# A hybrid attention layer on one core: the attention's work given out in pieces of one bank, and the q/k transposes spread over the gates' matmuls

## The chip, the core and the metric

The kernel runs on one core of one Trainium2 chip. The metric is the time of the whole launch in microseconds (us); lower is better. The kernel before took 1259.9 us, the median of three runs (1257.29 to 1260.52).

The engines are named as the profile names them: PE does matmuls (PEld loads their weights), DVE and ACT do element-wise work and read the matmuls' results, POOL does element-wise work on the core's own memory (SBUF), and SP issues nearly all transfers (DMA). Each has a queue of instructions and takes them in order. Matmul results stand in eight banks of 2 KB per partition (PSUM).

## The reference

One decoder layer over a sequence of 2048 tokens with a width of 1024, in float32: RMS norm, one input projection, two attention mixers with a SiLU gate each, an output projection and a residual.

```python
hdn = rmsnorm(x, norm_gain[i])
proj = jnp.einsum("bsd,de->bse", hdn, w_in[i])
q_a, k_a, v_a, g_a, q_b, k_b, v_b, g_b = jnp.split(proj, split_at, axis=-1)
# A: 8 query heads, 2 key heads: causal window of 128, with a learned sink per head
q_a = rope(rmsnorm(q_a, q_norm_a), pos); k_a = rope(rmsnorm(k_a, k_norm_a), pos)
o_a = banded_attention(q_a, k_a, v_a, A_WINDOW - 1, sinks) * jax.nn.silu(g_a)
# B: 8 heads, each under the patterns (128,1), (512,4), (2048,16), merged by denominators
q_b = rope(rmsnorm(q_b, q_norm_b), pos); k_b = rope(rmsnorm(k_b, k_norm_b), pos)
o_b = dilated_attention(q_b, k_b, v_b) * jax.nn.silu(g_b)
x = x + jnp.einsum("bse,ed->bsd", jnp.concatenate([o_a, o_b], -1), w_out[i])
```

## The kernel before, in words

**Stages and slots.** `STAGES` (L26) lists eight stages: four pairs of heads of mixer B, two groups of four heads of mixer A, and two column halves of the output projection. Each is cut into four slots of 512 tokens, a slot into two halves of 256. `proj(si, sb)` (L246) does the projection of one slot: for each half two groups of 8 x 3 matmuls for q, k and v (`pj`, tiles of 128x384), then the gates (8 x 3 matmuls per group, the second loop, L319). Each float32 product is three matmuls, of high and low parts (`mm3`, L241): weights `wh`, `wl`, activations `xh`, `xl`, gate weights `wgh`, `wgl`. ACT makes the high part and DVE or POOL the low one. In the last slot of a stage the next stage's weights are loaded into three staging buffers `stg` (L118, L131) and split by ACT and DVE (L104, L105).

**After a group of q, k, v**: `norm_rope` (L406) reads `pj` with ACT (squares, v) and DVE (rotary products t1, t2, and V at L311); POOL adds t1 and t2 (L431). `norm_factors` (L434) makes the norm factor `fac` on POOL (L437, L182). `norm_split` (L441) multiplies by it on DVE (L447) and splits into `hl` on ACT and POOL (L456 to L459). `finish` (L342) transposes `hl` on PE (`qk_transposes`: L475, L485, L490, L499), copies the results by ACT to Q, KK and `klz` (L477, L478, L502), and for B writes them to DRAM from the second half on (qd, kd, ld). Then it puts the slot's attention units in `pending`. `finish` is put in `deferred` at the end of a half and run in the next half, after the second group's matmuls (L305).

**Attention units.** A unit is one head on 512 queries: the windows of A and B (`window_unit`, `pair_units`), and for B the residue classes of the dilated pattern (`units_D`), which load q, k and v back from DRAM in another order (`load`). A unit has steps: scores (q times k, two or three banks `sc`; DVE adds the mask and takes the row maximum, ACT makes P, the exponentials, with row sums), transposes of P (banks `pt`; ACT copies the high part `pth`, DVE makes the low part `ptl`, both at `split_p`, L572), pv (the products of P with V, bank `po`, high parts, then low ones; ACT and DVE take the result), and after. `sc`, `pt`, `po` and `pj` have two banks each. After a dilated unit of the second head, row factors go to DRAM (rD) and come back spread over partitions (`Rb`, one buffer, L890); POOL then does four operations of 128x512: L899 (waits for the first `Rb`), L904 (waits for the second), L905, L906. These are put in `late`, with a count of steps to wait. A's `final` does the like (rA, L686, L688).

**What sets the order.** `proj` is a generator: it yields a cost after each 3 or 6 matmuls. The main loop (L968) calls `advance()` as often as the attention's share of cost asks for. `advance` (L931) moves the `late` counts on by one and gives out one step of one unit, in rounds over the units in flight: the oldest unit's step first, and of the newest its scores. The framework takes the order in which the code emits instructions as a priority and then orders each engine's queue by a timeline of its own.

Of the kernel before, what the change touches and what calls it, by code (L numbers as in the profile page):

```python
# [9 lines left out]
F32 = mybir.dt.float32  # L10
# [23 lines left out]
def hybrid_layer(ctx, tc, xT, xn, x, wB, wA, wO, ng, gains, sinks, rot, masks, ident, out):  # L34
# [211 lines left out]
    def proj(si, sb):  # L246
# [22 lines left out]
        for half in range(2):  # L269
# [8 lines left out]
            for tt in range(2):  # L278
# [40 lines left out]
            for gc in range(ngc):  # L319
                pg = ps.tile([128, 256], F32, name="pt" if early else "pj", bufs=2)  # L320
                for c in range(KC):
# [7 lines left out]
                    yield 330  # L329
                z = G[si, sb][gc][:, :, 2 * half:2 * half + 2, :]  # L330
# [185 lines left out]
    def proj_out(si, sb, wq, wg, last):  # L516
# [4 lines left out]
        for half in range(2):  # L521
# [6 lines left out]
            for tt in range(2):  # L528
# [20 lines left out]
                while deferred:  # L549
                    yield from deferred.pop(0)()  # L550
# [12 lines left out]

    def evac_o(po, dst):
# [11 lines left out]
    def window_scores(si, sb, h, nb, l):  # L576
# [4 lines left out]
        P = wk.tile([128, 4, 256], F32, name="P")  # L581
        for b in range(2):
# [19 lines left out]
    def window_unit(si, sb, h, stats, dst, after):  # L602
        s = {}

        def scores():
            s["p"] = window_scores(si, sb, h, *stats)
# [4 lines left out]
        def transposes():  # L611
            f0 = sb == 0
            cur0 = (0, 0) if f0 else (0, 1)
            n1, n2 = pt_slot()
            sp = spec
            s["n"], s["sp"] = (n1, n2), sp
            pt = ps.tile([128, 4, 128], F32, name="pt", bufs=2)
            for b, a in enumerate((cur0, (1, 0), (1, 1), (2, 0))):
                nc.tensor.transpose(pt[:, b, :], blk(*a), idf)
            split_p(pt, n1, n2)  # L620
# [7 lines left out]
        def pv():  # L628
            po = ps.tile([128, 512], F32, name="po", bufs=2)
# [7 lines left out]
            for hl in range(2):  # L637
                seq.append((v(0), n[hl][:, 0:2, :], 0))
                seq.append((v(1), n[hl][:, 2:4, :], 128))
                if sb > 0:  # L640
                    seq.append((v(-1), sp[hl][:, 1:6:4, :], 0))
                seq.append((v(2), sp[hl][:, 2:4, :], 256))
                seq.append((v(3), sp[hl][:, 0:5:4, :], 256))
            for n_, (a, b, o) in enumerate(seq):
                nc.tensor.matmul(po[:, o:o + 256], a, b, start=n_ == 0, stop=n_ == len(seq) - 1, skip_group_check=True)  # L645
            evac_o(po, dst)
# [393 lines left out]
```

## Time and profile before

| | |
|---|---|
| median of three runs | 1259.9 us |
| profiled execution, its own time | 1261.51 us |
| profiled execution, span from first to last instruction | 1259.4 us |
| PE busy, matmuls | 1174.8 us, 93%, 8328 |
| DVE, ACT, POOL busy | 850.7, 834.7, 680.4 us |
| mean granted clock of PE | 0.969 |
| DMA: moved, mean rate | 220.98 MB, 175 GB/s |

The page of the profile has a chain of waits (what ended last, followed back), groups of instructions by line, and the waits of each engine: whom it waited for, in total, how often, and the longest. In a row of the timeline the number in brackets is the engine's idle time ahead of the instruction, with what ended it. The granted clock is the share of full speed at which PE was allowed to run.

### The profile page before, as it was taken

How to read it: one execution, taken by the hardware profiler on the slowest of the kernel's cores; microseconds unless marked ns; L12 is line 12 of the kernel's file. 1: busy time of each engine (PE TensorE's matmuls, PEld its weight loads, DVE VectorE, ACT ScalarE, POOL GpSimd, SP SyncE). 2: the span in 40 equal slices, each digit the busy share in tenths (PEclk: the TensorE clock that was granted, in tenths of full speed). 3: DMA queues.
4: the chain of work that ended last, by engine and by line, in shares of the span. 5: the costliest groups of instructions: out<-in, count | busy, mean ns of one | idle time of the engine just before them, and what ended most of it. 6: DMA issues, size and time to landing. Idle time of an engine off the chain costs nothing.

```text
span 1259.4 us, 25438 instructions
## 1 busy us (share of the span) xinstructions
PE 1174.8 (93%) x8328; PEld 1141.3 (91%) x8328; DVE 850.7 (68%) x2288; ACT 834.7 (66%) x2418; POOL 680.4 (54%) x788
## 2 busy tenths in 40 slices
PE   6898979899899798899998999999999999999899
PEld 5898979899799798888997999898899998999898
DVE  5676768678677678776777788789868877522221
ACT  6477868678677687676777677677776776522221
POOL 4886734566645574536576567565655554333122
PEclk9899989999899899899998999999999999999999
DMA  7454677877687667687775764545333225566561
GB/s 215 120 166 127 193 226 212 229 200 212 182 250 207 210 190 201 189 244 204 199 210 172 228 203 143 150 137 167 114 97 94 80 89 165 163 192 211 166 191 69
DMA packets 196883, 220.98 MB, mean 175 GB/s; under 512 B 34312, under 2 KB 143632, under 8 KB 196752
## 3 DMA queue, kind: packets, MB, share of 16 engines
q1 hardware_dynamic: 196752, 219.37, 59.3%
q8 instruction: 66, 1.08, 0.4%
q14 instruction: 65, 0.53, 0.1%
HBM read 164.44 MB, written 54.86 MB: 174 GB/s over the span
## 4 chain that ended last, share of the span: by engine, by line
PE 55%; DMA 16%; DVE 10%; ACT 8%; POOL 6%; issue 3%; SPq 2%; POOLq 0%; ACTq 0%; DVEq 0%
PE pj L244 39%; DMA xs<-in_xT 3%; DMA Rb<-rD 2%; DMA stg<-in_wB 2%; PE po L849 2%; DMA stg<-in_wO 2%; DMA stg<-in_wA 2%; PE sc L590 1%; PE sc L591 1%; PE po L645 1%; PE pt L828 1%; PE po L735 1%; PE pt L719 1%; ACT P L599 1%; DVE ptl L574 1%
## 5 line engine op out<-in xcount | busy, mean ns | idle before, releaser
L244 PE MATMUL pj<-wh,xh 128*128 128x384 f32 (+1 forms) x1008 | 332.8, 332 | 12.2 <-ACT wh L104 5.5
L244 PE MATMUL pj<-wl,xh 128*128 128x384 f32 (+1 forms) x1008 | 334.4, 332 | 0.8 <-DVE wl L102 0.7
L244 PE MATMUL pj<-wh,xl 128*128 128x384 f32 (+1 forms) x1008 | 333.4, 331 | 1.3 <-DVE xl L157 1.3
L157 POOL TENSOR_TENSOR xl<-xs,xh 128x512 fp32r<-128x512 f32 x158 | 210.3, 1341 | 146.3 <-ACT xh L155 136.6
L155 ACT ACTIVATE xh<-xs 128x512 fp32r<-128x512 f32 x252 | 154.5, 629 | 123.6 <-PE pj L244 100.6
L244 PEld LDWEIGHTS pj<-wh,xh 128*128 128x128 f32 x1008 | 194.0, 193 | 15.7 <-ACT wh L104 5.8
L244 PEld LDWEIGHTS pj<-wl,xh 128*128 128x128 f32 x1008 | 194.8, 193 | 3.2 <-DVE wl L102 1.1
L244 PEld LDWEIGHTS pj<-wh,xl 128*128 128x128 f32 x1008 | 194.4, 193 | 3.0 <-DVE xl L157 1.6
L574 DVE TENSOR_TENSOR ptl<-pt,pth 128x512 fp32r<-128x512 f32 (+3 forms) x232 | 142.0, 619 | 35.5 <-ACT pth L573 31.8
L244 PE MATMUL pj<-xh,wgh 128*128 128x256 f32 x496 | 147.7, 298 | 17.9 <-DVE V L311 12.0
L244 PE MATMUL pj<-xh,wgl 128*128 128x256 f32 x496 | 145.8, 294 | 0.0
L244 PE MATMUL pj<-xl,wgh 128*128 128x256 f32 x496 | 145.4, 293 | 0.0
L573 ACT ACTIVATE pth<-pt 128x512 fp32r<-128x512 f32 (+3 forms) x232 | 123.1, 543 | 23.1 <-PE pt L719 8.1
L431 POOL TENSOR_TENSOR t<-t,t 128x256 f32<-128x256 f32 (+1 forms) x96 | 78.1, 814 | 77.9 <-DVE t L422 57.2
L244 PEld LDWEIGHTS pj<-xh,wgh 128*128 128x128 f32 x496 | 97.8, 197 | 19.7 <-ACT klz L502 5.9
L244 PEld LDWEIGHTS pj<-xl,wgh 128*128 128x128 f32 x496 | 97.8, 197 | 0.6
L244 PEld LDWEIGHTS pj<-xh,wgl 128*128 128x128 f32 x496 | 97.4, 196 | 0.9 <-DVE wgl L105 0.2
L814 ACT ACTIVATE P<-P,scD 128x256 f32<-128x256 f32 (+3 forms) x128 | 71.6, 560 | 33.6 <-DVE scD L813 32.9
L157 DVE TENSOR_TENSOR xl<-xs,xh 128x512 fp32r<-128x512 f32 x94 | 76.9, 823 | 21.1 <-ACT xh L155 20.5
L447 DVE TENSOR_TENSOR t<-t,fac 128x256 f32<-128x256 f32 (+1 forms) x96 | 67.4, 710 | 30.8 <-POOL fac L182 23.7
L182 POOL TENSOR_TENSOR fac<-un,mhalf 128x8 f32<-128x8 f32 (+1 forms) x48 | 85.4, 1779 | 2.5
L813 DVE CUSTOM_DVE_ANT_0 P<-sc,mk 128x256 f32<-128x256 f32 (+3 forms) x128 | 61.1, 484 | 32.2 <-PE sc L809 31.5
(188 smaller groups left out, 3082.8 us busy)
## 6 DMA issues: line engine op xcount, KB each, us to landing
xs<-in_xT SPq DMA_DIRECT2D x94, 512.0 KB
xs<-mx SPq DMA_DIRECT2D x32, 512.0 KB
vd<-V SPq DMA_DIRECT2D x64, 128.0 KB
qd<-qc SPq DMA_DIRECT2D x32, 256.0 KB
TT<-tab SPq DMA_DIRECT2D x32, 256.0 KB
cv<-vd SPq DMA_DIRECT2D x32, 256.0 KB
cq<-qd SPq DMA_DIRECT2D x32, 256.0 KB
ck<-kd SPq DMA_DIRECT2D x64, 128.0 KB
```

The costliest lines, as they stand in the source:

```text
L155: nc.scalar.activation(h, f, AF.Copy)
L157: eng.tensor_tensor(l, f, f32(h), op=OP.subtract)
L182: nc.gpsimd.tensor_tensor(y, u, mhalf.to_broadcast([128, n]), op=OP.pow)
L244: nc.tensor.matmul(o, a, b, start=first and n == 0, stop=last and n == 2, skip_group_check=True)
L431: nc.gpsimd.tensor_tensor(t1[:, :n], t1[:, :n], t2[:, :n], op=OP.add)
L447: nc.vector.tensor_tensor(t1v, t1v, fac[:, tt, :, None].to_broadcast([128, nh, 64]), op=OP.mult)
L573: nc.scalar.activation(hi, pt, AF.Copy)
L574: nc.vector.tensor_tensor(lo, pt, f32(hi), op=OP.subtract)
L590: nc.tensor.matmul(sc[:, j, :], q[h // 2][:, h % 2, i, :], kw, start=True, stop=False)
L813: nc.vector.tensor_tensor_reduce(pd, o[:, :m], m2[:, 512 - m:], -0.125, BIG, OP.add, OP.min, nb)
L814: nc.scalar.activation(pd, pd, AF.Exp, bias=nb, scale=-1.0, accum_out=l)
L849: nc.tensor.matmul(po[:, o:o + w], a, b, start=n_ == 0, stop=n_ == len(seq) - 1, skip_group_check=True)
```

## The change

`finish` is now a generator of which `fin_step()` takes one part at a time: four parts for a half of B (two banks of q/k transposes, the bank of low parts of k, the end), taken after every second group of gate matmuls instead of all at once after the second q/k/v group. What is left is taken before `norm_split`. In the output stages it is taken between the matmuls too.

A unit's step is now a list of parts of one bank each (`parts`): scores 2 (dilated: 3), transposes 2 (3), pv 2 (high parts, low parts). `advance` gives out one part. It makes up a round as: pv and after of the older units, then two banks of transposes, then the first bank of scores, the third bank of transposes, and the rest of the scores. The counts in `late` are the same numbers, now counted in parts. The order of the products in pv changes (high parts of all blocks, then low parts, the preceding block last). The instructions are the same and as many.

```diff
@@ proj @@
                 if tt == 1:
                     if si == 0 and hf < 7:
                         rstd(hf + 1)
-                    while deferred:
-                        yield from deferred.pop(0)()
...
                     yield 330
+                    if c % 2 == 0:
+                        yield fin_step()
...
+            while deferred:
+                yield fin_step()
             hls = norm_split(kind, nq, nk, t1s, fac)
             if si == 0 and hf < 7:
                 rb_make(hf + 1)
-            deferred.append(lambda half=half, hls=hls: finish(si, sb, half, hls))
+            deferred.append(finish(si, sb, half, hls))
+
+    def fin_step():
+        if deferred:
+            for cost in deferred[0]:
+                return cost
+            deferred.pop(0)
+        return 0
...
+    def parts(fn, *costs):
+        return [(lambda n=n: fn(n), c) for n, c in enumerate(costs)]
+
@@ window_unit @@
-        return [(scores, 870), (transposes, 870), (pv, 1090), (after, 60)]
+        return [parts(scores, 435, 435), parts(transposes, 435, 435), parts(pv, 545, 545), [(after, 60)]]
@@ units_D @@
-            return [(scores, 1194), (transposes, 1090), (pv, 1194), (after, 60), load]
+            return [parts(scores, 434, 326, 434), parts(transposes, 436, 327, 327), parts(pv, 597, 597), [(after, 60)], load]
@@ advance @@
-            todo.extend(pipe)
+            seqs = []
+            for ent in pipe[:]:
+                seqs.append((ent[1], ent[0][ent[1]]))
+                ent[1] += 1
+                if ent[1] == len(ent[0]):
+                    pipe.remove(ent)
+            for n, q in seqs:
+                if n > 1:
+                    todo.extend(q)
+            t = [x for n, q in seqs if n == 1 for x in q]
+            sc = [x for n, q in seqs if n == 0 for x in q]
+            if t:
+                todo.extend(t[:2])
+                if len(t) > 2:
+                    todo.extend(sc[:1] + t[2:])
+                    sc = sc[1:]
+            todo.extend(sc)
         if not todo:
-            return None
-        ent = todo.pop(0)
-        fn, cost = ent[0][ent[1]]
+            return 0
+        fn, cost = todo.pop(0)
         fn()
-        ent[1] += 1
-        if ent[1] == len(ent[0]):
-            pipe.remove(ent)
         return cost
```

Three places show how the instructions move; line numbers differ between the two kernels. The first is POOL's queue in the fourth stage, ahead of one half's norm factor `fac`. Before (L899, L904 to L906 are the four late operations of a dilated unit):

```order
L904 TENSOR_TENSOR osum<-osum,Rb 128x512
L458 TENSOR_TENSOR hl<-t_7965,hl 128x128
L459 TENSOR_TENSOR hl<-t_7965,hl 128x128
L905 TENSOR_TENSOR osum<-osum,o1c 128x512
L906 TENSOR_TENSOR osum<-osum,gc 128x512
L437 TENSOR_TENSOR un<-un,eps_84 128x8
L182 TENSOR_TENSOR fac<-un,mhalf 128x8
```

And now (L920, L925 to L927 are the same four operations):

```order
L920 TENSOR_TENSOR o1c<-o1c,Rb 128x512
L467 TENSOR_TENSOR hl<-t_7920,hl 128x128
L468 TENSOR_TENSOR hl<-t_7920,hl 128x128
L467 TENSOR_TENSOR hl<-t_7981,hl 128x128
L468 TENSOR_TENSOR hl<-t_7981,hl 128x128
L446 TENSOR_TENSOR un<-un,eps_84 128x8
L182 TENSOR_TENSOR fac<-un,mhalf 128x8
L440 TENSOR_TENSOR t_8306<-t_8306,t_8307 128x256
L925 TENSOR_TENSOR osum<-osum,Rb 128x512
L926 TENSOR_TENSOR osum<-osum,o1c 128x512
```

The second, third and fourth late operation moved from ahead of `fac` to behind it; the first, which waits for a transfer, stands ahead of it. In an earlier half of the third stage the same exchange stands closer, before:

```order
L459 TENSOR_TENSOR hl<-t_5470,hl 128x128
L905 TENSOR_TENSOR osum<-osum,o1c 128x512
L437 TENSOR_TENSOR un<-un,eps_84 128x8
L906 TENSOR_TENSOR osum<-osum,gc 128x512
L182 TENSOR_TENSOR fac<-un,mhalf 128x8
```

and now:

```order
L488 CAST qc<-Q 128x8x32
L920 TENSOR_TENSOR o1c<-o1c,Rb 128x512
L446 TENSOR_TENSOR un<-un,eps_84 128x8
L488 CAST qc<-Q 128x8x32
L182 TENSOR_TENSOR fac<-un,mhalf 128x8
```

Two additions left the place ahead of `fac`, and the product that waits for `Rb` came in.

The second place is PE's queue in the third stage's first slot, where one window unit is ended (L590 and L591 are scores, L619 and L625 transposes of P, L645 products). Before:

```order
L590 MATMUL sc<-KK,Q 128x256
L591 MATMUL sc<-klz_90,Q 128x256
L645 MATMUL po<-pth,V 128x256 x3
L645 MATMUL po<-ptl,V 128x256 x5
L625 MATMUL pt<-idf,P 128x128
L619 MATMUL pt<-idf,P 128x128
L625 MATMUL pt<-idf,P 128x128 x3
L645 MATMUL po<-pth,V 128x256 x2
L244 MATMUL pj<-wh,xh 128x384
```

And now (L603 and L604 scores, L632 and L640 transposes; 21 more rows of L244 are left out):

```order
L603 MATMUL sc<-KK,Q 128x256
L604 MATMUL sc<-klz_90,Q 128x256
L244 MATMUL pj<-wh,xh 128x384
L244 MATMUL pj<-wl,xh 128x384
...
L632 MATMUL pt<-idf,P 128x128
L640 MATMUL pt<-idf,P 128x128
L244 MATMUL pj<-wh,xl 128x384
L640 MATMUL pt<-idf,P 128x128 x2
L244 MATMUL pj<-xh,wgh 128x256
```

Between the last scores and the transposes stood eight products; now 23 projection matmuls stand there.

The third place is PE's queue at the end of the third stage, from the last transposes of the low parts of k (L499, now L508), after which q and k are written to DRAM, to the first scores of a dilated unit that loads them back (L808, now L830). Before, with 78 matmuls between them:

```order
L475 MATMUL po_7248<-idr_76,hl_7145 128x128 x4
L499 MATMUL po_7256<-idr_76,hl_7139 128x128
L499 MATMUL po_7256<-idr_76,hl_7145 128x128
L244 MATMUL pj_7498<-wh_6958,xh_7184 128x384
...
L244 MATMUL pj_7580<-wl_7017,xh_7449 128x384
L808 MATMUL sc_7507<-ck_7359,cq_7357 128x256
L808 MATMUL sc_7516<-ck_7359,cq_7357 128x384
L809 MATMUL sc_7507<-cl_7362,cq_7357 128x256
```

And now, with 51 between them:

```order
L508 MATMUL po_7326<-idr_76,hl_7170 128x128
L508 MATMUL po_7326<-idr_76,hl_7176 128x128
L603 MATMUL sc_7381<-KK_6499,Q_6497 128x256
L603 MATMUL sc_7420<-KK_6499,Q_6497 128x256
...
L640 MATMUL pt_7412<-idf_75,P_7371 128x128 x2
L830 MATMUL sc_7478<-ck_7392,cq_7390 128x256
L830 MATMUL sc_7490<-ck_7392,cq_7390 128x384
L831 MATMUL sc_7478<-cl_7395,cq_7390 128x256
```

The transposes of the low parts of k, now a part of their own, stand later, and the loads' first use stays.

More of the change, by code (lines that the diff above doesn't have):

```diff
@@ L820, in blk, with transposes @@
                 return s["p"][:, o:o + 128]
-            def transposes():
-                s["n"] = []
-                for kt in range(2):
+            def transposes(part):
+                if part < 2:
+                    kt = part
                     n1, n2 = pt_slot()
@@ L963, in hybrid_layer @@
             pending.extend(units_D(si - 1, sb))
-        left = sum(c for e in pipe for _, c in e[0][e[1]:])
+        left = sum(c for _, c in todo) + sum(c for e in pipe for st_ in e[0][e[1]:] for _, c in st_)
         own = {"B": 4 * 2900, "A": 4 * 2600, "O": 0}[kind] if n else 0
-        total = left + sum(st_[1] for u in pending for st_ in u if not callable(st_)) + own
+        total = left + sum(c for u in pending for st_ in u if not callable(st_) for _, c in st_) + own
         done = pr = 0.0
@@ L969, in hybrid_layer @@
             pr += cost
-            while (pending or pipe) and done < total * pr / pcost[kind]:
-                if not pending and len(pipe) <= 2 and kind != "O":
+            while (pending or pipe or todo) and done < total * pr / pcost[kind]:
+                if not pending and len(pipe) <= 2 and kind != "O" and not todo:
                     break
@@ L974, in hybrid_layer @@
         if kind == "O":
-            while pending or pipe:
+            while pending or pipe or todo:
                 advance()
```

141 lines of the change are left out of this document (75 added, 66 removed).

## The prediction

> **What bounds the kernel now.** I read the page's busy times and chain first, then PE's waits, the windows of 40 us, and the timeline around the longest waits. The head of the page, the chain by engine, and the costliest group:
>
> ```profile
> span 1259.4 us, 25438 instructions
> PE 1174.8 (93%) x8328; PEld 1141.3 (91%) x8328; DVE 850.7 (68%) x2288; ACT 834.7 (66%) x2418; POOL 680.4 (54%) x788
> PE 55%; DMA 16%; DVE 10%; ACT 8%; POOL 6%; issue 3%; SPq 2%; POOLq 0%; ACTq 0%; DVEq 0%
> L244 PE MATMUL pj<-wh,xh 128*128 128x384 f32 (+1 forms) x1008 | 332.8, 332 | 12.2 <-ACT wh L104 5.5
> ```
>
> PE is the engine that sets the end: busy 93%, idle 1259.4 - 1174.8 = 84.6 us. The change removes no instruction, so the time can move only by those 84.6 us and by the clock. The chain passes through DMA, DVE, ACT and POOL wherever PE waits. PE's waits (whom, total us, times, longest us):
>
> ```profile
> PE pj L244 <- DVE V L311: 13.2, 7, 5.7
> PE sc L591 <- ACT klz L502: 5.8, 2, 4.7
> PE pt L828 <- DVE ptl L574: 5.2, 2, 5.0
> PE po L499 <- ACT KK L478: 4.8, 1, 4.8
> PE pj L244 <- ACT KK L478: 4.6, 1, 4.6
> PE pt L619 <- DVE ptl L574: 2.7, 1, 2.7
> PE po L475 <- POOL hl L458: 2.6, 1, 2.6
> PE sc L590 <- DVE scD L813: 1.8, 1, 1.8
> PE sc L808 <- DMA ck<-kd: 1.6, 1, 1.6
> PE sc L808 <- DVE scD L813: 1.3, 1, 1.3
> PE pj L244 <- DVE xl L157: 1.3, 1, 1.3
> ```
>
> Few and long: not a constant trickle of short waits, but some dozen events. What each costs beyond itself shows in five windows (busy PE, PEld, DVE, ACT, POOL, then the granted clock):
>
> ```profile
> 200.00:240.00 40.00, 40.00 (x281) 39.04 (x280) 29.76 (x91) 31.43 (x95) 17.64 (x23) 1.00 0.73 213
> 240.00:280.00 40.00, 36.77 (x249) 35.41 (x247) 28.27 (x77) 28.53 (x82) 25.16 (x31) 0.96 0.81 214
> 400.00:440.00 40.00, 32.32 (x202) 30.91 (x201) 24.55 (x61) 24.62 (x76) 27.50 (x33) 0.87 0.74 217
> 480.00:520.00 40.00, 32.91 (x216) 31.76 (x215) 29.07 (x62) 27.10 (x74) 22.05 (x25) 0.87 0.63 175
> 800.00:840.00 40.00, 39.95 (x302) 38.74 (x300) 33.74 (x101) 33.60 (x104) 26.02 (x29) 1.00 0.42 132
> ```
>
> From 240 to 280 us PE idles 3.2 us, 2.6 of it in one wait, and the clock is 0.96: 0.04 x 40 = 1.6 us more. From 400 to 440 us it idles 7.7 us and loses 0.13 x 40 = 5.2 us of clock. I price a wait of some 1.5 us or more at itself plus 1.6 us.
>
> What makes the long waits? Around 400 us, POOL and DVE:
>
> ```profile
> 394.85 1.29 POOL L899 TENSOR_TENSOR o1c<-o1c,Rb 128x512 f32<-128x512 f32 x1 [8.23 <-DMA Rb<-rD]
> 399.75 1.29 POOL L904 TENSOR_TENSOR osum<-osum,Rb 128x512 f32<-128x512 f32 x1 [1.61 <-DMA Rb<-rD]
> 402.70 1.29 POOL L905 TENSOR_TENSOR osum<-osum,o1c 128x512 f32<-128x512 f32 x1
> 404.11 1.28 POOL L906 TENSOR_TENSOR osum<-osum,gc 128x512 f32<-128x512 f32 x1
> 405.35 1.64 POOL L182 TENSOR_TENSOR fac<-un,mhalf 128x8 f32<-128x8 f32 x1
> 407.03 2.37 DVE L447 TENSOR_TENSOR t<-t,fac 128x256 f32<-128x256 f32 x2 [4.64 <-POOL fac L182]
> ```
>
> The norm factor stands in POOL's queue behind late work of a dilated unit. DVE's product L447 waits 4.64 us for it at the head of DVE's queue, and `ptl`, which PE needs, waits behind L447: that is the 2.7 us of L619. The 5.0 us of L828 is the same thing some 23 us later. The chain from 578 us shows it once more (start, duration), ahead of the two waits of 1.3 us:
>
> ```profile
> 578.42 1.28 POOL osum L906
> 579.94 1.66 POOL fac L182
> 584.18 1.49 DVE t L447
> ```
>
> The other class stands at the ends of the B stages, where ACT waits for weights and the copies of q and k stand behind it:
>
> ```profile
> 157.64 5.71 DMA stg<-in_wB
> 165.43 0.27 ACT KK L478
> ```
>
> **The change, part by part.** The sum is made against the profiled execution (1261.5 us, 2.1 beyond its span), 1.6 above the median of 1259.9, so I subtract from the median.
>
> (1) POOL's late work ahead of `fac`. Over the 48 factors, counted in POOL's queue, the late operations among the last three ahead of a factor fall from 24 to 14. Six of the waits above are of this class (both of `scD`, both of `ptl`, `hl`, `xl`): 5.2 + 2.7 + 2.6 + 1.8 + 1.3 + 1.3 = 14.9 us, and with four slow windows of 1.6 it is 21.3. Ten of 24 parts of that is -8.9. The half shown first is an instance: L905 and L906 go behind `fac`, 2 x 1.28 us, as much as its two waits of 1.3. Against this, two halves of the third stage get the product that waits for `Rb` ahead of their factor, and that wait was 1.6 to 8.2 us: at a chance of 0.45 each of one event of 2.7 + 1.6, +3.9. Together -5; bounds: -21 (the whole class) and +13 (three new events of 2.7 + 1.6).
>
> (2) Room between dependent pieces. Priced at a projection matmul's rate of
>
> ```profile
> 67.38 4.16 PE pj L244 x24
> ```
>
> 4.16 / 24 = 0.173 us, the matmuls that stand between the last PE instruction behind a wait and the waiting one can be counted. Under 2 us of room had 76 waits, and now 51; of transposes that wait for P, 11 and now 3. In the place shown 23 x 0.173 = 4.0 us of projection now cover the mask, the maximum and the exponentials. The waits that this touches are short ones:
>
> ```profile
> PE pt L625 <- ACT P L599: 1.3, 2, 0.7
> PE pt L619 <- ACT P L599: 1.1, 2, 0.6
> PE po L645 <- ACT pth L573: 0.8, 2, 0.5
> PE pt L835 <- DVE ptl L574: 0.7, 1, 0.7
> ```
>
> 3.9 us, of which 8/11 go: -2.8, and one slow window of 1.6 that three of them made together near 346 us: -4. Bounds 0 (the queue heads decide, not the room) and -5.5.
>
> (3) The q/k transposes. Their number is the same; the copies (0.27 us each) now stand between the gate weights' splits on ACT at the four stage ends. Before, they stood there as well (KK behind all four pairs at the first end). The loads, the three staging buffers and SP's order of them are as before, so the waits of 4.6 to 5.7 us stay: 0. Below, -5 if one such wait finds its copy ahead of the load; above, +13 if two further copies come to stand behind a load (2 x (4.8 + 1.6)).
>
> (4) The first dilated unit of a stage. Its q and k go to DRAM after the last transposes and come back. Before:
>
> ```profile
> 513.45 0.33 PE L499 MATMUL po<-idr,hl 128*128 128x128 f32 x2
> 523.52 3.51 DMA cq<-qd
> ```
>
> From 513.45 to the landing at 527.03 is 13.6 us, covered by 78 matmuls. Now 51 stand there: 51/78 x 13.6 = 8.9 us, 4.7 us short, 6.3 with the slow window. At the other three stage ends the count goes 62 to 64, 77 to 66 and 88 to 71; the first had a wait of 1.6. Since the low parts alone come later and q's and k's loads stand a little earlier on SP, I take two thirds: +4. Bounds 0 and +13 (two ends).
>
> (5) Nothing else moves on the path: the projection, the loads of x and the stores are the same, and DVE and ACT get the same instructions. pv's new order of products costs nothing.
>
> Sum: -5 - 4 + 0 + 4 = -5 us, 1259.9 - 5 = 1255 us, a ratio of 1.004. About 0.3%, 3.8 us, is what a measurement of this kernel can tell from no change, so the forecast lies just beyond.
>
> **A rule that speaks against the change.** From 800 to 840 us 302 matmuls of all kinds, transposes among them, ran with a clock of 1.00 and 0.05 us idle; only windows with waits show less. The Trainium skill ("Perfetto Trace Analysis", Matmul Optimizations) says that matmuls should run back to back in batches, because PE's power follows its use; its "TensorE: Matmul & The Clock Gate" (Part 4: PE-mode transpose) adds that transposes do not count as such use. By these, shorter pieces would cost clock. The row of 800 to 840 us does not bear it out.
>
> **The rivals.**
>
> - A, the long waits go: the whole of (1) (21.3) and of (2) (4.4), with (4) at 0: 1259.9 - 26 = 1234. For it: late operations near `fac` fall by 10 of 24. Against: two halves exchange them for the `Rb` wait.
> - B, no change: the queue heads (a DMA, `fac`, a weight split) make all waits of weight and the new order only deals them out anew; (1) at 0, (2) -4, (4) +4: 1260. For it: of the 48.8 us in the two lists of waits, the short ones that a bank's room can close are 3.9.
> - C, slower: POOL's product with `Rb` stands ahead of `fac`. The `late` counts now run in parts, so the broadcast is asked for sooner after the factors are written, and the product enters POOL's queue while its transfer is under way. In four halves a DVE wait as at 407 us (4.64 us), which PE feels as 5.0 + 1.6: 4 x 6.6 = +26 in place of (1), with (2) and (4) as above; the 5.0 and 2.7 of before go into it, with their clock: 26 - 11 = +15, 1275. It decides from three such halves on (+9).
> - D, slower: the weights' waits at the stage ends grow as in (3)'s upper bound: -5 + 13 = +8, 1268.
> - E, shorter pieces cost clock: one more slow window of 1.6 us in each of the 24 slots of the attention stages, +38: 1298. This is what the skill's rule above would give.
> - F, the transposes stay bunched, because the framework's own timeline decides the order: then (2) falls and it is B. The order shown speaks against it.
>
> **Chances.** Forecast 0.42 (its own range 1246 to 1258, a tenth of its chance within 0.3%), A 0.12, B 0.21, C 0.13, D 0.10, E 0.02. Faster by over 0.3%: 0.38 + 0.12 = 0.50; within: 0.21 + 0.04 = 0.25; slower: 0.25. For 8 in 10 the range takes in most of A (from 1237) and D, and stops short of C: 1237 to 1270.
>
> **What would show it.** (1): L447 on DVE waits less for `fac` than now, and the wait on `xl` (1.3) is gone; a wait of L447 behind L920 says C. (2): PE's waits on P (L612) sum to under 1 us. (3): waits of 4 to 6 us behind weight splits are still there, four to six of them; more say D. (4): PE waits for ck, cq or cl of the dilated loads, some 4 us at one stage end. The mean clock goes from 0.969 to about 0.972. I am wrong if PE's idle time changes by over 15 us, or if the clock moves without the idle time.

## The result, and the profile after

The changed kernel takes 1279.0 us (median, 1274.8 to 1281.4), the kernel before 1260.2 beside it: a ratio of 1.0146 with a 95% interval of 1.0111 to 1.0182. The change makes the kernel slower, by 18.8 us. The forecast was 1255; rival C, POOL's product with `Rb` ahead of the factor, had 1275.

The head of the page and the chain by engine of the changed kernel (its profiled run took 1274.8 us, the shortest of its four):

```profile
span 1273.0 us, 25489 instructions
PE 1178.9 (93%) x8328; PEld 1140.4 (90%) x8328; DVE 863.1 (68%) x2288; ACT 834.6 (66%) x2418; POOL 682.3 (54%) x788
PE 54%; DMA 15%; DVE 15%; ACT 7%; POOL 4%; issue 3%; SPq 2%; DVEq 0%; ACTq 0%; POOLq 0%
```

PE's idle time is 1273.0 - 1178.9 = 94.1 us, 9.5 more than before, and its busy time is 4.1 longer. DVE's share of the chain went from 10 to 15%, the largest move. PE's waits, those that answer to the list of before and the longest on a weight split (whom, total us, times, longest):

```profile
PE pj L244 <- DVE G L332: 11.0, 3, 5.5
PE sc L604 <- ACT klz L511: 7.9, 3, 3.6
PE po L661 <- DVE ptl L586: 7.6, 3, 6.8
PE po L484 <- POOL hl L467: 7.4, 3, 3.4
PE pj L244 <- ACT wh L104: 6.3, 2, 5.4
PE pt L856 <- DVE ptl L586: 5.4, 2, 3.8
PE pj L244 <- DVE V L309: 4.8, 6, 1.2
PE sc L831 <- DMA cl<-ld: 2.4, 3, 1.5
PE sc L830 <- DMA ck<-kd: 1.2, 1, 1.2
PE pt L632 <- ACT P L612: 0.3, 1, 0.3
```

Waits on `V` shrank (13.2 before) and waits on P are nearly gone. The ones that grew stand on DVE's `G` (3.2 before) and `ptl` (5.2 and 2.7 before) and on POOL's `hl` (2.6 before). What is behind these shows in DVE's own list of waits, in the row of its product with the norm factor. Before, and then after:

```profile
DVE t L447 <- POOL fac L182: 23.7, 9, 5.7
```

```profile
DVE t L456 <- POOL fac L182: 47.8, 14, 7.8
```

It doubled. POOL's timeline at the longest of the 14, factor 13 of 0 to 47 (start, duration; in brackets idle time and what ended it):

```profile
267.77 0.73 POOL L440 TENSOR_TENSOR t<-t,t 128x256 f32<-128x256 f32 x1 [3.56 <-DVE t L431]
280.76 1.27 POOL L920 TENSOR_TENSOR o1c<-o1c,Rb 128x512 f32<-128x512 f32 x1 [12.26 <-DMA sd<-scB]
281.99 0.20 POOL L446 TENSOR_TENSOR un<-un,eps 128x8 f32<-128x8 f32 x1
282.15 0.72 POOL L440 TENSOR_TENSOR t<-t,t 128x256 f32<-128x256 f32 x1
282.83 1.65 POOL L182 TENSOR_TENSOR fac<-un,mhalf 128x8 f32<-128x8 f32 x1
```

DVE's timeline at the same place, and PE's:

```profile
284.50 2.00 DVE L456 TENSOR_TENSOR t<-t,fac 128x256 f32<-128x256 f32 x2 [7.76 <-POOL fac L182]
286.43 0.41 DVE L332 TENSOR_TENSOR G<-pj,RB 128x256 f32<-128x256 f32 x1
```

```profile
281.06 0.34 PE L244 MATMUL pj<-wl,xh 128*128 128x384 f32 x1
286.89 0.69 PE L244 MATMUL pj<-wh,xh 128*128 128x384 f32 x1 [5.50 <-DVE G L332]
287.38 0.52 PE L244 MATMUL pj<-wl,xh 128*128 128x384 f32 x1
```

POOL stands 12.26 us at the head of its queue with a product that waits for a broadcast. (The row names `sd<-scB`, a transfer that uses the same semaphore as an older operand of the product; in the trace the second half of the broadcast landed at 280.60 us, 0.16 us ahead of the product.) The factor's three instructions are queued behind it, DVE stands at L456, the gates' product L332 stands behind that, and with it the bank that PE needs next. After PE's 5.50 us a matmul of the same shape lasts 0.52 us instead of 0.34: the slow clock that follows an idle stretch. The chain of waits at that place says where the 12 us went:

```profile
270.87 6.12 DMA rD<-rr
277.01 0.47 SPq L911
279.26 1.51 DMA sd<-scB
280.77 1.26 POOL o1c L920
```

The store of the row factors to DRAM takes 6.12 us, only then are the two halves of the first broadcast issued (L911), and the product starts 9.9 us after the store was issued. The stretch from 280 to 320 us, in the windows (busy PE, PEld, DVE, ACT, POOL, then the clock), before and after:

```profile
280.00:320.00 40.00, 39.94 (x279) 38.99 (x278) 32.71 (x86) 33.70 (x97) 26.74 (x31) 1.00 0.68 197
```

```profile
280.00:320.00 40.00, 34.51 (x222) 33.60 (x221) 27.54 (x76) 27.41 (x82) 27.55 (x33) 0.91 0.58 175
```

57 matmuls fewer fit in. Worked out from the two traces, factor by factor: a product with `Rb` that made POOL idle stood between the factor's input and the factor, with a DVE wait of over 1 us behind it, at factors 12, 19, 20, 27 and 28 before, and at 11, 13, 19, 20, 27, 28 and 35 after. Before, these were the second product (POOL idle 1.6 to 3.8 us there), at one of them the first as well (7.3). After, six of the seven have the first product, whose transfer comes behind the store of rD, and POOL idled 5.9 to 12.3 us there.

POOL waited for the first product before the change too:

```profile
POOL o1c L899 <- DMA Rb<-rD: 58.3, 15, 8.2
```

With idle time of every name, POOL stood idle ahead of all sixteen first products in both kernels, 60.5 us before and 75.6 us after. The waits grew by a quarter; what is new is that six of them cost a factor's wait of over 1 us, where one did before.

### The profile page after: what moved, and what is told of

Same layout as the page of the kernel before. It is cut to its first block, busy times and chain, and to the rows that moved or that the text cites. A ratio compares the mean times of both kernels' runs of the same rounds, so it can differ in the third digit from the quotient of the medians.

```text
span 1273.0 us, 25489 instructions
## 1 busy us (share of the span) xinstructions
PE 1178.9 (93%) x8328; PEld 1140.4 (90%) x8328; DVE 863.1 (68%) x2288; ACT 834.6 (66%) x2418; POOL 682.3 (54%) x788
## 4 chain that ended last, share of the span: by engine, by line
PE 54%; DMA 15%; DVE 15%; ACT 7%; POOL 4%; issue 3%; SPq 2%; DVEq 0%; ACTq 0%; POOLq 0%
PE pj L244 37%; DMA Rb<-rD 2%; PE po L867 2%; DMA stg<-in_wB 2%; DVE xl L157 2%; DVE t L456 2%; PE po L661 2%; DVE ptl L586 2%; DVE P L611 2%; DMA stg<-in_wO 2%; ACT P L612 1%; DMA cl<-ld 1%; PE po L755 1%; DMA xs<-in_xT 1%; PE pt L738 1%
## 5 line engine op out<-in xcount | busy, mean ns | idle before, releaser
L244 PE MATMUL pj<-wh,xh 128*128 128x384 f32 (+1 forms) x1008 | 333.2, 333 | 20.7 <-DVE G L332 10.0
L244 PE MATMUL pj<-wl,xh 128*128 128x384 f32 (+1 forms) x1008 | 333.5, 331 | 1.7 <-DVE wl L105 1.0
L244 PE MATMUL pj<-wh,xl 128*128 128x384 f32 (+1 forms) x1008 | 332.8, 331 | 0.2 <-DVE xl L157 0.2
L157 POOL TENSOR_TENSOR xl<-xs,xh 128x512 fp32r<-128x512 f32 x158 | 213.0, 1358 | 156.6 <-ACT xh L155 151.7
L244 PEld LDWEIGHTS pj<-wh,xh 128*128 128x128 f32 x1008 | 192.9, 192 | 24.7 <-DVE G L332 11.1
L244 PEld LDWEIGHTS pj<-wl,xh 128*128 128x128 f32 x1008 | 193.3, 192 | 3.9 <-DVE wl L105 1.7
L244 PEld LDWEIGHTS pj<-wh,xl 128*128 128x128 f32 x1008 | 193.3, 192 | 2.2 <-DVE xl L157 1.2
L244 PE MATMUL pj<-xh,wgh 128*128 128x256 f32 x496 | 148.4, 299 | 7.3 <-DVE V L309 2.7
L244 PE MATMUL pj<-xl,wgh 128*128 128x256 f32 x496 | 145.9, 294 | 0.0
L244 PE MATMUL pj<-xh,wgl 128*128 128x256 f32 x496 | 145.7, 294 | 0.0
L585 ACT ACTIVATE pth<-pt 128x512 fp32r<-128x512 f32 (+3 forms) x232 | 122.9, 543 | 24.7 <-PE pt L738 10.6
L244 PEld LDWEIGHTS pj<-xh,wgh 128*128 128x128 f32 x496 | 97.8, 197 | 9.4 <-ACT wgh L104 5.4
L456 DVE TENSOR_TENSOR t<-t,fac 128x256 f32<-128x256 f32 (+1 forms) x96 | 71.8, 760 | 49.6 <-POOL fac L182 47.8
L244 PEld LDWEIGHTS pj<-xl,wgh 128*128 128x128 f32 x496 | 98.1, 198 | 0.8
L244 PEld LDWEIGHTS pj<-xh,wgl 128*128 128x128 f32 x496 | 97.7, 197 | 0.8 <-DVE wgl L105 0.2
L836 ACT ACTIVATE P<-P,scD 128x128 f32<-128x128 f32 (+3 forms) x128 | 71.8, 561 | 37.5 <-DVE scD L835 36.7
L157 DVE TENSOR_TENSOR xl<-xs,xh 128x512 fp32r<-128x512 f32 x94 | 80.0, 858 | 20.2 <-ACT xh L155 19.6
L835 DVE CUSTOM_DVE_ANT_0 P<-sc,mk 128x128 f32<-128x128 f32 (+3 forms) x128 | 61.0, 481 | 28.7 <-PE sc L831 26.9
```

The lines of the kernel that those rows point to most:

```text
L157: eng.tensor_tensor(l, f, f32(h), op=OP.subtract)
L244: nc.tensor.matmul(o, a, b, start=first and n == 0, stop=last and n == 2, skip_group_check=True)
L456: nc.vector.tensor_tensor(t1v, t1v, fac[:, tt, :, None].to_broadcast([128, nh, 64]), op=OP.mult)
L585: nc.scalar.activation(hi, pt, AF.Copy)
L835: nc.vector.tensor_tensor_reduce(pd, o[:, :m], m2[:, 512 - m:], -0.125, BIG, OP.add, OP.min, nb)
L836: nc.scalar.activation(pd, pd, AF.Exp, bias=nb, scale=-1.0, accum_out=l)
```

## The experiments

Theory S: what the change loses is this stall, POOL's wait for a transfer ahead of the norm factor. Its main rivals: Q, the spread q/k transposes; P, that smaller pieces cost by themselves; L, that any edit makes the framework order all queues anew, and where a late product falls is chance.

All results first. "Cured" is a kernel with this stall taken away, and "same, other pacing" the one above it with two constants changed that should not matter; both are shown below. The clock is the mean granted one. "Waits for fac" is DVE's row as above (us, times). "PE idle behind" is worked out from the trace: PE's idle stretches of over 0.2 us from the moment DVE begins to wait 0.8 us or more for a factor until 14 us after its product starts. The last four columns are of one profiled execution each, which need not be the median one: that of "q/k only" was its longest (1268.2 us), those of "before, three `t1`" and "counts doubled" their shortest (1254.2 and 1258.4).

| kernel | us | ratio to before | clock | waits for fac | PE idle | PE idle behind |
|---|---|---|---|---|---|---|
| before | 1260.2 | | 0.969 | 23.7, 9 | 84.6 | 13.8 |
| the change | 1279.0 | 1.0146 (1.0111 to 1.0182) | 0.970 | 47.8, 14 | 94.1 | 31.0 |
| pieces only | 1271.9 | 1.0095 (1.0064 to 1.0126) | 0.964 | 52.4, 16 | 94.4 | 33.8 |
| q/k only | 1263.1 | 1.0038 (1.0012 to 1.0064) | 0.969 | 38.8, 13 | 90.2 | 24.2 |
| the change, counts doubled | 1269.6 | 1.0107 (1.0070 to 1.0144) | 0.977 | 37.0, 13 | 82.6 | 19.1 |
| the change, three `t1` | 1269.6 | 1.0079 (1.0052 to 1.0106) | 0.974 | 31.9, 14 | 90.1 | 17.2 |
| before, three `t1` | 1259.3 | 1.0016 (0.9990 to 1.0042) | 0.971 | 18.4, 11 | 80.4 | 10.8 |
| the change, two `Rb` | 1243.4 | 0.9884 (0.9848 to 0.9921) | 0.982 | 32.2, 13 | 73.3 | 14.3 |
| the change, cured | 1235.3 | 0.9815 (0.9773 to 0.9857) | 0.979 | 3.4, 4 | 63.6 | 0.4 |
| same, other pacing | 1235.7 | 0.9837 (0.9798 to 0.9877) | 0.980 | 10.6, 9 | 62.7 | 2.7 |
| pieces only, cured | 1241.1 | 0.9846 (0.9796 to 0.9895) | 0.975 | 14.3, 11 | 72.1 | 2.8 |
| same, other pacing | 1237.0 | 0.9819 (0.9781 to 0.9858) | 0.981 | 13.0, 11 | 71.5 | 3.9 |
| size of pieces only, cured | 1240.8 | 0.9856 (0.9825 to 0.9887) | 0.975 | 13.1, 11 | 68.5 | 4.5 |
| new order only, cured | 1242.6 | 0.9884 (0.9835 to 0.9933) | 0.977 | 11.9, 9 | 72.2 | 4.5 |
| q/k only, cured | 1243.7 | 0.9899 (0.9869 to 0.9930) | 0.981 | 12.9, 7 | 74.2 | 6.4 |
| same, other pacing | 1229.0 | 0.9764 (0.9740 to 0.9788) | 0.979 | 9.1, 6 | 62.0 | 3.1 |
| before, cured | 1225.1 | 0.9741 (0.9700 to 0.9782) | 0.976 | 5.4, 4 | 64.6 | 2.8 |
| same, other pacing | 1227.0 | 0.9761 (0.9728 to 0.9794) | 0.976 | 5.7, 4 | 60.0 | 2.4 |

The kernel before took 1256.6 to 1260.2 us in these comparisons.

**One part of the change at a time.** q/k only: the kernel before, with this of the change.

```diff
-                    while deferred:
-                        yield from deferred.pop(0)()
...
                     yield 330
+                    if c % 2 == 0:
+                        yield fin_step()
```

> The kernel before, with one part of the change: the q/k transposes of a half are given out bank by bank between the gates' matmuls; the attention steps stay whole and in the old order. Theory S (the change's loss is POOL holding up the norm factors: POOL stands at a product with Rb that waits for its transfer, the factor is queued behind it, DVE's product with the factor waits; all of it brought by the attention pieces): little moves, 1255 to 1266 us, DVE's waits for fac stay near the 23.7 us of before. Rival Q (the spread transposes hold ACT and POOL up and bring the loss): 1272 or more. Rival L (any edit reshuffles the queues, and where a product falls ahead of a factor is chance): anything from 1250 to 1280, with the time following DVE's waits for fac.

Measured: 1263.1 us, 38.8 us of waits for `fac`. The time is within S's range, the waits are not: they grew by 15 us without any piece. That is L's picture, with a small price.

Pieces only: the changed kernel, with these lines taken back.

```diff
+                    while deferred:
+                        yield from deferred.pop(0)()
...
                     yield 330
-                    if c % 2 == 0:
-                        yield fin_step()
```

> The changed kernel, with the q/k transposes given out as before (all of a half at once, after the next half's second product group). Theory S: the pieces bring the loss, so 1270 to 1285 us, DVE's waits for fac 40 us or more (23.7 before, 47.8 with the whole change). Rival Q (the spread transposes bring it): 1263 or less. Rival L: anything from 1250 to 1280, with the time following DVE's waits for fac.

Measured: 1271.9 us and 52.4 us, as S has it. Q is out as the cause of the loss.

**The stall taken away.** Both broadcasts of a dilated pair are asked for at once, and the four products go into POOL's queue together, behind the last split of a half (`issue_after` orders a queue, it waits for nothing).

```diff
-        t1 = wk.tile([128, 320], F32, name="t1", bufs=4)
+        t1 = wk.tile([128, 320], F32, name="t1", bufs=3)
...
-            rb = wk.tile([128, 512], F32, name="Rb", bufs=1)
+            rb = wk.tile([128, 512], F32, name="Rb", bufs=2)
...
-                    rb = bcast(0)
-                    late.append([3, lambda: second(rb)])
+                    rb, rb2 = bcast(0), bcast(1)
+                    behind.append(lambda: second(rb, rb2))
...
-                    rb = bcast(1)
-                    late.append([3, lambda: third(rb)])
+                    third(rb2)
...
+    def flush(ins):
+        while behind:
+            with tc.issue_after(ins):
+                behind.pop(0)()
...
             hls = norm_split(kind, nq, nk, t1s, fac)
+            flush(hold[0])
...
-            nc.gpsimd.tensor_tensor(klo, t1v[:, nq:], f32(khi[:, :, 0, :]), op=OP.subtract)
+            hold[0] = nc.gpsimd.tensor_tensor(klo, t1v[:, nq:], f32(khi[:, :, 0, :]), op=OP.subtract).ins
```

> The changed kernel, with the price of POOL's stall taken away: both Rb broadcasts of a dilated pair are asked for at once (two Rb buffers, one t1 buffer fewer to make the room), and the four POOL products of the pair are queued in one go right behind the splits of a half, a whole half ahead of the next factor. Theory S: DVE's waits for fac fall from 47.8 to 15 us or less (the 3 us at the start stay), the time to 1235 to 1255 us, below the kernel before. Rival P (the smaller pieces cost by themselves: more changes of kind on PE, shorter stretches, clock): the waits go, but the time stays at 1265 or more.

Measured: 1235.3 us, 43.7 less than the change without the cure. Waits and time are as S has them, and P's 1265 is out. The head of the page and POOL's timeline at the same half:

```profile
span 1233.6 us, 25461 instructions
PE 1170.0 (95%) x8328; PEld 1135.3 (92%) x8328; DVE 863.9 (70%) x2288; ACT 831.7 (67%) x2418; POOL 681.2 (55%) x788
```

```profile
265.05 0.20 POOL L455 TENSOR_TENSOR un<-un,eps 128x8 f32<-128x8 f32 x1 [3.34 <-DVE un L431]
265.33 1.65 POOL L182 TENSOR_TENSOR fac<-un,mhalf 128x8 f32<-128x8 f32 x1
...
279.46 0.45 POOL L477 TENSOR_TENSOR hl<-t,hl 128x128 fp32r<-128x128 f32 x1
279.87 1.29 POOL L930 TENSOR_TENSOR o1c<-o1c,Rb 128x512 f32<-128x512 f32 x1
281.13 1.28 POOL L934 TENSOR_TENSOR osum<-osum,Rb 128x512 f32<-128x512 f32 x1
282.49 1.31 POOL L935 TENSOR_TENSOR osum<-osum,o1c 128x512 f32<-128x512 f32 x1
283.88 1.29 POOL L936 TENSOR_TENSOR osum<-osum,gc 128x512 f32<-128x512 f32 x1
```

POOL now does nothing between the factor's input and the factor, and the four products run behind the split without a gap: the broadcasts had landed. DVE's row shrank to

```profile
DVE t L465 <- POOL fac L182: 3.4, 4, 1.4
```

By the two profiled runs the span fell by 39.4 us: PE's idle time by 94.1 - 63.6 = 30.5, all but the same as what stood behind the waits for `fac` (31.0 - 0.4 = 30.6), and its busy time by 8.9, with the clock up from 0.970 to 0.979.

The same cure on the kernel before:

> The kernel before, with the same cure as in the run on the changed kernel: both Rb broadcasts asked for at once (two Rb buffers, three t1 buffers), and the four late POOL products queued right behind the splits of a half. Theory S: DVE's waits for fac fall from 23.7 to some 4 us and the time by about as much, to 1235 to 1248 us; what then is left between this and 1235.3 is what the change is worth without the stall (small, by the short waits on P it removes: 2 to 5 us). Rival W (the cure works only together with the pieces, which give the products room): 1255 or more. Rival N (with the stall gone the change is worth nothing, or is a loss): 1236 or less.

Measured: 1225.1 us, ratio 0.9741, the fastest of all the kernels here, and below S's 1235 to 1248. Rival N: with the stall gone the change is not worth anything, it is 10 us behind. Its page and DVE's row:

```profile
span 1228.2 us, 25461 instructions
PE 1163.6 (95%) x8328; PEld 1135.9 (92%) x8328; DVE 871.0 (71%) x2288; ACT 835.8 (68%) x2418; POOL 679.9 (55%) x788
```

```profile
DVE t L456 <- POOL fac L182: 5.4, 4, 2.9
```

The cure is worth 32.5 us here, far more than the 13.8 us of PE's idle time that stood behind the waits for `fac`. By the profiled runs the span fell by 31.2 us: 11.0 of idle time behind these waits, 9.0 of other idle time, and 11.2 of busy time. So the cure does more than take this stall away, and its full gain must not be booked to the stall.

What separates the two cured kernels is PE's busy time: 1170.0 against 1163.6 us, with all but the same idle time (63.6 and 64.6). Counted at full rate (busy time less half of what fell into stretches at half clock), PE is busy 4.5 to 7.6 us longer with the change in each of the four pairs that differ in nothing else: before and the change, the two with three `t1`, the two cured, and the two cured with the other pacing.

**Half of the cure.** Two buffers and both broadcasts at once, but the products where the framework puts them:

```diff
-                    rb = bcast(0)
-                    late.append([3, lambda: second(rb)])
+                    rb, rb2 = bcast(0), bcast(1)
+                    late.append([3, lambda: second(rb, rb2)])
...
-                    rb = bcast(1)
-                    late.append([3, lambda: third(rb)])
+                    late.append([3, lambda: third(rb2)])
```

> The changed kernel with half of the cure: both Rb broadcasts asked for at once (two Rb buffers, three t1 buffers), while the products stay where the framework queues them, with the late counts of the change. Theory S with the transfer as the cause of the stall, the place in the queue as what makes it cost: the second product's waits (25.4 us in all) go, the first's (60.2 us) stay, so DVE's waits for fac fall only partly, 15 to 35 us, and the time is 1247 to 1268. Rival D (one buffer too few is the whole cause): under 10 us of waits and 1233 to 1243.

Measured: 1243.4 us with 32.2 us of waits for `fac`: the waits as S has them, the time below S's range. POOL's waits for broadcasts in this kernel, and in the changed one:

```profile
POOL o1c L920 <- DMA Rb<-rD: 61.6, 15, 7.8
```

```profile
POOL o1c L920 <- DMA Rb<-rD: 37.5, 9, 8.9
POOL osum L925 <- DMA Rb<-rD: 25.4, 8, 5.2
POOL o1c L920 <- DMA sd<-scB: 22.7, 3, 12.3
```

The second product's waits are gone, the first's are as they were (61.6 against 37.5 + 22.7). Where they fall is not as it was, since the framework ordered the queue anew. So DVE's waits are not the price: PE felt 14.3 us behind 32.2 here, 31.0 behind 47.8 in the changed kernel. By the profiled runs the span is 32.0 us shorter than the change's: 20.8 of idle time (16.7 of it behind the waits for `fac`) and 11.2 of busy time, at a clock of 0.982. This half alone brings 35.6 of the cure's 43.7 us. The other half, the place behind the split with one buffer, was not run, so the gain is not divided between the two.

**Controls.** The `t1` buffers that paid for the second `Rb`, alone, first on the changed kernel and then on the kernel before:

```diff
-        t1 = wk.tile([128, 320], F32, name="t1", bufs=4)
+        t1 = wk.tile([128, 320], F32, name="t1", bufs=3)
```

> A control: the changed kernel with three t1 buffers instead of four, and nothing else. A t1 buffer is free again a whole half before its fourth successor needs it, so by waits this is worth nothing; but the framework orders every queue anew. Theory S: 1279, within 4 us, unless the number of products ahead of a factor happens to move. Rival L (where the late products fall is chance): 1255 to 1290, and the time follows DVE's waits for fac (47.8 us in the changed kernel).

> The control on the other side: the kernel before with three t1 buffers instead of four. By waits it is worth nothing; the queues are ordered anew. If the time follows DVE's waits for fac as in the runs so far (23.7 us: 1259; 31.9: 1270; 38.8: 1263; 47.8: 1279; 52.4: 1272; 3.4: 1235), it lies within 8 us of 1237 plus 0.85 us for each us of these waits, whatever they come to; without a link it is 1259, within 4.

Measured: 1269.6 and 1259.3 us. The first moved by 9 us, and its PE idle time behind the factors from 31.0 to 17.2: rival L is at work. The second did not move in time, with waits for `fac` of 18.4, which the line asked for puts at 1253: within its 8 us, but no better than no link at all. Neither comes near the cured kernels.

**The late counts.** The prediction's rival C had said why the product comes early: the counts in `late` now run in parts.

```diff
-                late.append([2, first])
+                late.append([4, first])
```

and likewise 3, 3 and 5 to 6, 6 and 10.

> The changed kernel with the late counts doubled (2, 3, 3, 5 become 4, 6, 6, 10), so that counted in parts they stand for the old numbers of steps. Theory K (the counts, which now run twice as fast, ask for the broadcasts too early and so put the products with Rb ahead of the factor, as the rival of the prediction said): DVE's waits for fac fall back to 20 to 28 us and the time to 1255 to 1264. Theory F (the framework queues a product where its own timeline has the broadcast landed, whatever the count; what the pieces changed is how POOL's and PE's work falls around it): waits of 35 us or more, PE's idle time right behind them 15 us or more, time 1268 to 1282.

Measured: 1269.6 us and 37.0 us of waits, 19.1 of PE idle time behind them (its profiled run, at 1258.4, was the shortest of six). That is theory F. The interval, 1.0070 to 1.0144, overlaps the change's own, and the control above moved as far without touching a count. The counts are not shown to matter.

**What is left with the stall gone.** q/k only and pieces only, each with the cure as above:

> The cured kernel before (both Rb broadcasts at once, products behind the splits), with the q/k transposes spread over the gates' matmuls; attention steps whole and in the old order. Cured so far: before 1225.1, pieces alone 1241.1, the whole change 1235.3. Theory G (the pieces cost some 10 us of their own, the spread transposes nothing): 1223 to 1230. Rival H (the differences among the cured kernels are the luck of a new order of the queues): anywhere from 1222 to 1242.

> The cured changed kernel (both broadcasts at once, products behind the splits) with the q/k transposes as before: all of a half at once, after the next half's second product group. Theory S: the stall is gone here too, DVE's waits for fac under 8 us, and the spread transposes are worth little: 1233 to 1242. Rival Q (the spread transposes carry the gain over the kernel before): 1245 or more.

Measured: 1243.7 and 1241.1 us. The first lies outside both of its ranges, and the second kernel's waits for `fac`, 14.3 us, are above the 8 that S had. Each alone has a higher median than both together (1235.3), which no sum of prices gives. So the pacing constants were changed a little, to have each of the four cured kernels once more with other queues:

```diff
-        own = {"B": 4 * 2900, "A": 4 * 2600, "O": 0}[kind] if n else 0
+        own = {"B": 4 * 3000, "A": 4 * 2700, "O": 0}[kind] if n else 0
```

> A control among the cured kernels: the whole change, cured, with the pacing constants of the attention (cost of a slot's own units) put from 2900 and 2600 to 3000 and 2700. By itself it is worth nothing, but the queues are ordered anew. Theory G (the pieces cost some 10 us of their own): 1232 to 1239. Rival H (luck of the order): 1222 to 1245.

> The same control on the cured kernel before: pacing constants 3000 and 2700. Theory G: 1221 to 1229, still some 10 us below the cured change. Rival H: 1220 to 1240.

> The control on the cured kernel with pieces and the new order (1241.1): pacing constants 3000 and 2700. If the 16 us over the cured kernel before are a cost of the part, 1236 to 1246; if they are the luck of one order of the queues, anywhere from 1225 to 1246.

> The control on the cured kernel with the spread q/k transposes alone (1243.7): pacing constants 3000 and 2700. If the 19 us over the cured kernel before are a cost of the part, 1239 to 1248; if they are luck, anywhere from 1225 to 1248.

Measured: 1235.7, 1227.0, 1237.0 and 1229.0 us. Three stay within about 4 us of their twins; q/k only falls by 15. So most of the 19 us of the first were luck of one order of the queues, and 15 us is what such luck can make. Last, the two halves of the pieces' part, each made from the cured kernel with pieces only by one of these edits: the new order of a round with whole steps, and one bank at a time in the old order. Both keep the change's order of the products in pv, so neither is the cured kernel before plus one thing alone.

```diff
-        return [(lambda n=n: fn(n), c) for n, c in enumerate(costs)]
+        return [(lambda: [fn(n) for n in range(len(costs))], sum(costs))]
```

```diff
-                if n > 1:
-                    todo.extend(q)
...
+                todo.extend(q)
```

> The cured kernel before, with the new order of a round alone: steps stay whole, but a round is given out as products first, then transposes, then scores. q/k transposes as before. Theory O (the new order costs: scores now come last in a round, and what DVE and ACT make of them is late for the next round's transposes): 1235 or more, with waits on P or pth/ptl in PE's list. Rival Z (the size of the pieces costs, more changes of kind on PE): 1222 to 1230 here.

> The cured kernel before, with the pieces alone: one bank at a time, the oldest unit first as before. Theory O: 1222 to 1230. Rival Z: 1235 or more, and PE's busy time outside the slow windows 1145 us or more (1140 in the cured kernel before, 1145 to 1148 with the whole change).

Measured: 1242.6 and 1240.8 us. Both are slow, so they don't tell order from size; PE's busy time at full rate is 1141.3 us in the first and 1143.3 in the second, where Z asked for 1145 or more. PE's waits on P and `pth`, which O asked for, are there in both: 9.0 and 9.5 us, against 0.3 in the cured kernel before. The six cured kernels with pieces or the new order lie at 1235.3 to 1242.6, the four without at 1225.1, 1227.0, 1229.0 and 1243.7. That speaks for a cost of some 10 us, with one exception out of four. Of it, the 5 to 8 us of PE's busy time come back in both cured pairs; the rest, with a luck of 15 us, stays open.

## Why the prediction was wrong

- **(1), -5, is the step that failed, in sign.** It read POOL's queue by "the late operations among the last three ahead of a factor fall from 24 to 14" and priced a wait by its share of that count. The count is right and says nothing: a product of 1.3 us whose operands are there and one that stands 12.26 us for its transfer count the same. What matters is which late operation is ahead of the factor. The text saw the product with `Rb` ahead in "two halves of the third stage" at a chance of 0.45 each; a product with `Rb` was ahead and cost DVE over 1 us in seven halves (five before), six of them with the first product (one before). PE's idle time behind the factors went from 13.8 to 31.0 us: +17.2 in place of -5. It was the largest term of the loss.
- **Rival C named the wait**, and its 1275 is 4 us from the 1279.0. That it came so close is luck: it took four halves at 6.6 us, and there were seven, with PE waits of 0.7 to 6.8 us behind them, 29.5 in all. Its clock share of 1.6 us each did not show in the mean clock (0.969 before, 0.970 after), and its reason, the counts, is not borne out. The order that the chance of 0.13 should have been read from was there: at factor 13 the product stood three places ahead of `fac`, inside the count of 14.
- **(2), -4, held in part.** Waits on P were 2.1 + 1.3 + 1.1 + 0.2 = 4.7 us and are 0.3. But waits on `pth`, of the same list, went from 0.8 to 2.8 us, so some 2.4 of the 4 are left.
- **(3), 0, was too careful.** The waits behind weight splits and copies (`V`, `klz`, `KK`, and after also `wgh` with 2.5) sum to 28.6 us before and 15.4 after; some of that went to other names, for PE's idle time in the first slot of stages two to five fell from 28.0 to 23.4. That -4.7 stands near its lower bound of -5. Its sign, four to six waits of 4 to 6 us behind weight splits, failed: of the five before, one is left (`wh`, 5.4).
- **(4), +4, was right in sign and too large**: waits for ck, cl and cq went from 2.1 to 3.6 us.
- **Busy time is a second step that failed.** The text let the time move only by idle time and by the clock, as no instruction is removed, and put the new order of products at nothing. Busy time grew by 4.1 us at a clock of 0.970 instead of the 0.972 foretold; at full rate it grew by 4.5, and by 5.4 to 7.6 in three more pairs of kernels with and without the change. So it comes with the change in all four; what holds it is open, for no group of matmuls does.
- **Rival E and the rule of the Trainium skill** ("Perfetto Trace Analysis", Matmul Optimizations: matmuls back to back in batches): the trace does not bear it out for these pieces. The cured change runs at a clock of 0.979 to 0.980, the cured kernel before at 0.976.

In the profiled runs the 13.6 us of span are thus +17.2 of idle time behind the factors, -7.7 of idle time elsewhere (9.5 - 17.2, of the size that (2) and (3) brought), and +4.1 of busy time. The runs without the stall say how far this carries: the cure brings 43.7 us in the changed kernel and 32.5 in the kernel before. These differ by 11 us, and that much of the 18.8 is shown to go with the cure; the other 8 to 10 us remain in both cured pairs, beside 5 to 8 us more of PE's busy time at full rate. As the order of the queues alone moved other kernels by up to 15 us, the division is no finer than that. That the change must put the product ahead of the factors is not shown either: with three `t1`, PE's idle time behind them falls from 31.0 to 17.2 us.

## What to carry to other kernels

Ahead of an instruction on the critical path, count the waits in its engine's queue, not the operations: one that stood 12.26 us for a transfer outweighed several of 1.3 us that were ready. Work that is late by nature belongs right behind the urgent instruction, with its transfers asked for well ahead of it; here the two together took 2.6% off the kernel before. And where a framework orders the queues, give a change a neutral twin before its parts are priced: neutral edits here moved the time by up to 15 us.

## What was not expected of the hardware

- A store of 8 KB (rD) took up to 6.12 us until it landed: 1.3 to 6.1 us in the changed kernel's trace, where the broadcast was seen to wait for it. The first product started 5.4 to 10.9 us after its store was issued (5.0 to 10.6 in the kernel before). Work that goes through DRAM and back on the way to POOL was 5 to 11 us away here, not one transfer.
- The half clock does not need an idle window. PE's clock falls to half for stretches of 3.41 us or a multiple. Cut into windows of that length and phase, the traces of the kernel before, the changed one and the cured kernel before have 28 windows at full clock, behind the start, in which PE idled 1.9 us or more; the clock was at half in the next in all 28. Of windows with 1.4 to 1.9 us it followed on some third (8 of 22), with 1.1 to 1.4 us on 2 of 14, below that on none. By these counts one may estimate that a wait of 2 us costs a stretch of 3.41 us at half speed, some 1.7 us more, where it falls within one window, and nothing where it straddles two. The Trainium skill ("TensorE: Matmul & The Clock Gate", Part 1) puts it at one idle window or more of about 3.4 us; here 1.9 us of idle time in it were enough. Such a pair of windows in the changed kernel, 2.5 us idle and then the clock at 0.5:

```profile
685.08:688.49 3.41, 0.93 (x7) 0.73 (x7) 2.29 (x8) 3.17 (x9) 2.56 (x3) 1.00 0.73 229
688.49:691.90 3.41, 3.41 (x17) 3.41 (x18) 3.41 (x6) 2.27 (x9) 3.41 (x4) 0.50 0.82 265
```
